# Instance norm over 268 MB of traffic: fp32 units kept on chip, with loads and stores in one queue

## The chip, the cores and the metric

The kernel runs on one core of a Trainium2 chip, and the other cores are idle. The metric is the device time of one execution in microseconds (us), as a median over several runs.

## The reference

```python
# x: (4, 8, 16, 256, 256) float32, gamma: (8, 16) float32
mu  = x.mean(axis=(3, 4), keepdims=True)
var = ((x - mu) ** 2).mean(axis=(3, 4), keepdims=True)
out = (x - mu) / np.sqrt(var + 1e-5) * gamma[None, :, :, None, None]
```

There are 512 channels of 65,536 values each. A channel has to be read whole before its first output is known. Since x is 134.22 MB and out is as large, at least 268.44 MB pass through the core's DMA engines, if x is read once.

## The kernel before

It takes 128 channels at a time, one to a partition. They come in as 2 MB pieces (rows of 16 KB) through four staging buffers. ACT copies each piece to a bf16 cache and sums it, and DVE sums its squares. When all 16 pieces are in, DVE scales the cache in place, and Pool issues stores that cast bf16 back to fp32.

```python
    # CW = 4096; staging has bufs=4; x_cache is [128, 65536] bf16, one buffer
    for ct in range(n_chtiles):                       # 4 tiles of 128 channels
        for j, (off, width) in enumerate(cur_p1):     # last tile ends in 4 pieces of 1024
            x_ck = staging.tile([P, CW], mybir.dt.float32, name="xck")
            nc.sync.dma_start(out=x_ck[:, :width], in_=x_flat[ch_lo:ch_hi, off : off + width])
            nc.scalar.activation(out=x_cache[:, off : off + width], in_=x_ck[:, :width],
                func=mybir.ActivationFunctionType.Copy, accum_out=sum_parts[:, j : j + 1])
            nc.vector.tensor_tensor_reduce(out=sq_scratch[:, :width], in0=x_ck[:, :width],
                in1=x_ck[:, :width], ..., accum_out=sq_parts[:, j : j + 1])
        # ... scale_ and shift_ from the sums: eight small instructions on DVE and ACT ...
        for j, (off, width) in enumerate(p2_chunks):  # 16 pieces
            nc.vector.tensor_scalar(out=x_cache[:, off : off + width], in0=..., scalar1=scale_[:],
                scalar2=shift_[:], op0=mybir.AluOpType.mult, op1=mybir.AluOpType.add)
            nc.gpsimd.dma_start(out=out_flat[ch_lo:ch_hi, off : off + width],
                                in_=x_cache[:, off : off + width])   # casts bf16 -> fp32
```

Of the kernel before, what the change touches and what calls it, by code (L numbers as in the profile page):

```python
# [1 line left out]

# [4 lines left out]


@with_exitstack  # L10
def kernel(
    ctx: ExitStack,
    tc: tile.TileContext,
    x: bass.AP,
    gamma: bass.AP,
    out: bass.AP,
):
    nc = tc.nc
    B, G, C, H, W = x.shape
    HW = H * W  # L20
    n_ch = B * G * C
    P = nc.NUM_PARTITIONS

    assert n_ch % P == 0
    assert G * C == P, "kernel assumes gamma broadcast exactly along partition dim"

    x_flat = x.rearrange("b g c h w -> (b g c) (h w)")
    out_flat = out.rearrange("b g c h w -> (b g c) (h w)")
    gamma_flat = gamma.rearrange("g c -> (g c)")

    n_chtiles = n_ch // P
    CW = 4096
    TAIL = 1024
    assert HW % CW == 0
    n_chunks = HW // CW
    p1_chunks = [(i * CW, CW) for i in range(n_chunks)]
    n_tail = CW // TAIL
    p1_chunks_last = [(i * CW, CW) for i in range(n_chunks - 1)] + [
        ((n_chunks - 1) * CW + i * TAIL, TAIL) for i in range(n_tail)
    ]  # L40
    p2_chunks = p1_chunks

    cache_dt = mybir.dt.bfloat16

    staging = ctx.enter_context(tc.tile_pool(name="staging", bufs=4))
    cache_pool = ctx.enter_context(tc.tile_pool(name="cache", bufs=1))
    singles = ctx.enter_context(tc.tile_pool(name="singles", bufs=1))
    scratch_pool = ctx.enter_context(tc.tile_pool(name="scratch", bufs=1))
    stats_pool = ctx.enter_context(tc.tile_pool(name="stats", bufs=2))

    g_tile = singles.tile([P, 1], mybir.dt.float32)
    nc.sync.dma_start(out=g_tile[:], in_=gamma_flat[:, None])  # L52

    eps_tile = singles.tile([P, 1], mybir.dt.float32)
    nc.vector.memset(eps_tile[:], 1e-5)  # L55

    x_cache = cache_pool.tile([P, HW], cache_dt)
    sq_scratch = scratch_pool.tile([P, CW], cache_dt)

    for ct in range(n_chtiles):  # L60
        ch_lo = ct * P
        ch_hi = ch_lo + P

        cur_p1 = p1_chunks_last if ct == n_chtiles - 1 else p1_chunks
        n_p1 = len(cur_p1)
        sum_parts = stats_pool.tile([P, n_p1], mybir.dt.float32, name="sum_parts")
        sq_parts = stats_pool.tile([P, n_p1], mybir.dt.float32, name="sq_parts")

        for j, (off, width) in enumerate(cur_p1):
            x_ck = staging.tile([P, CW], mybir.dt.float32, name="xck")  # L70
            nc.sync.dma_start(  # L71
                out=x_ck[:, :width], in_=x_flat[ch_lo:ch_hi, off : off + width]
            )
            nc.scalar.activation(  # L74
                out=x_cache[:, off : off + width],
                in_=x_ck[:, :width],
                func=mybir.ActivationFunctionType.Copy,
                accum_out=sum_parts[:, j : j + 1],
            )
            nc.vector.tensor_tensor_reduce(  # L80
                out=sq_scratch[:, :width],
                in0=x_ck[:, :width],
                in1=x_ck[:, :width],
                scale=1.0,
                scalar=0.0,
                op0=mybir.AluOpType.mult,
                op1=mybir.AluOpType.add,
                accum_out=sq_parts[:, j : j + 1],
            )

        sum_ = stats_pool.tile([P, 1], mybir.dt.float32, name="sum_")
        sq_sum_ = stats_pool.tile([P, 1], mybir.dt.float32, name="sq_sum_")
        nc.vector.reduce_sum(out=sum_[:], in_=sum_parts[:], axis=mybir.AxisListType.X)  # L93
        nc.vector.reduce_sum(out=sq_sum_[:], in_=sq_parts[:], axis=mybir.AxisListType.X)

        inv_n = 1.0 / HW
        tmp_ = stats_pool.tile([P, 1], mybir.dt.float32, name="tmp_")
        nc.vector.tensor_scalar(  # L98
            out=tmp_[:],
            in0=sum_[:],  # L100
            scalar1=sum_[:],
            scalar2=-inv_n,
            op0=mybir.AluOpType.mult,
            op1=mybir.AluOpType.mult,
        )
        nc.vector.tensor_add(out=sq_sum_[:], in0=sq_sum_[:], in1=tmp_[:])  # L106
        rstd_ = stats_pool.tile([P, 1], mybir.dt.float32, name="rstd")
        nc.scalar.activation(  # L108
            out=rstd_[:],
            in_=sq_sum_[:],  # L110
            func=mybir.ActivationFunctionType.Sqrt,
            bias=eps_tile[:],
            scale=inv_n,
        )
        nc.vector.reciprocal(out=rstd_[:], in_=rstd_[:])  # L115
        scale_ = stats_pool.tile([P, 1], mybir.dt.float32, name="scale")
        nc.vector.tensor_mul(out=scale_[:], in0=rstd_[:], in1=g_tile[:])  # L117
        shift_ = stats_pool.tile([P, 1], mybir.dt.float32, name="shift")
        nc.vector.tensor_scalar(  # L119
            out=shift_[:],  # L120
            in0=sum_[:],
            scalar1=-inv_n,
            scalar2=scale_[:],
            op0=mybir.AluOpType.mult,
            op1=mybir.AluOpType.mult,
        )

        for j, (off, width) in enumerate(p2_chunks):
            nc.vector.tensor_scalar(  # L129
                out=x_cache[:, off : off + width],  # L130
                in0=x_cache[:, off : off + width],
                scalar1=scale_[:],
                scalar2=shift_[:],
                op0=mybir.AluOpType.mult,
                op1=mybir.AluOpType.add,
            )
            nc.gpsimd.dma_start(  # L137
                out=out_flat[ch_lo:ch_hi, off : off + width],
                in_=x_cache[:, off : off + width],
            )  # L140


# [1 line left out]
_INS = ['x', 'gamma']  # L144
_OUTS = [((4, 8, 16, 256, 256), 'float32')]


# [23 lines left out]
```

## Time and profile before

| | before |
|---|---|
| measured, median of 3 runs (us) | 643.14 |
| span of the profile (us) | 641.5 |
| bytes over the DMA (MB) | 268.49 |
| DMA rate, loads only / both directions / stores only (GB/s) | 429 / 428 / 431 |
| DVE, ACT busy (share of the span) | 58%, 38% |

The first view is the page of the kernel before. The rows of digits have one place for each of 40 equal slices of the span, and a 9 means busy for 90% or more. GB/s is what the DMA engines moved in each slice. The last lines are groups of instructions: line, engine, operation, output<-input, count, then busy time and mean duration in ns, then the idle time just before them and what ended most of it.

```profile
span 641.5 us, 779 instructions
...
DVE 369.2 (58%) x227; ACT 241.7 (38%) x140; POOL 60.2 (9%) x68
...
DMA  8999999999999999999999999999999999599997
GB/s 355 429 430 428 429 426 430 430 429 426 431 428 427 429 427 433 431 427 430 428 429 427 427 429 429 392 440 425 426 426 433 431 425 426 230 425 441 425 436 316
...
q1 hardware_dynamic: 9792, 134.22, 55.0%
q0 software_dynamic: 9216, 134.22, 50.6%
...
L80 DVE CUSTOM_DVE_ANT_0 sq_scratch<-xck 128x4096 bf16<-128x4096 f32 (+1 forms) x67 | 283.6, 4233 | 201.5 <-DMA xck<-in_x_dram 201.0
L74 ACT ACTIVATE x_cache<-xck 128x4096 bf16<-128x4096 f32 (+1 forms) x67 | 232.0, 3463 | 301.4 <-issue 161.1
```

The DMA row is full almost everywhere, and the compute engines mostly wait for data: of DVE's 201.5 us of idle time before its square pass, a load ended 201.0. So the DMA engines bound the kernel.

The next view is a table of windows of the kernel before: from:to and length in us, busy time of DVE, ACT and Pool with instruction counts, the clock, the DMA share, and GB/s in the last column.

```profile
20.00:80.00 60.00, 54.47 (x25) 45.78 (x25) 0.00 (x0) 1.00 1.01 429
140.00:240.00 100.00, 46.32 (x21) 37.09 (x20) 1.59 (x3) 1.00 1.10 428
552.00:560.00 8.00, 7.28 (x16) 3.15 (x7) 1.67 (x2) 1.00 0.13 53
580.00:620.00 40.00, 0.00 (x0) 0.00 (x0) 2.65 (x5) 1.00 1.06 431
```

The rate hardly depends on the direction. In the third window the DMA share is 0.13: the engines have nothing to do for 7 of 8 us. The timeline of the kernel before (start, length, engine, line, operation, and in brackets the idle time before) says why:

```profile
553.38 1.22 DVE L80 CUSTOM_DVE_ANT_0 sq_scratch<-xck 128x1024 bf16<-128x1024 f32 x1
...
555.54 0.29 ACT L108 ACTIVATE rstd<-sq_sum__491,eps_tile 128x1 f32<-128x1 f32 x1 [0.68 <-DVE sq_sum__491 L106]
...
558.15 1.08 POOL L137 DMA_DIRECT2D out_dram<-x_cache  x1 [78.15 <-DVE x_cache L129]
```

The loads are over, and the last squares, the coefficients and the first scaled piece have to be done before the first store of the last tile can be issued at 558.15.

### The profile page before, as it was taken

How to read it: one execution, taken by the hardware profiler on the slowest of the kernel's cores; microseconds unless marked ns; L12 is line 12 of the kernel's file. 1: busy time of each engine (PE TensorE's matmuls, PEld its weight loads, DVE VectorE, ACT ScalarE, POOL GpSimd, SP SyncE). 2: the span in 40 equal slices, each digit the busy share in tenths (PEclk: the TensorE clock that was granted, in tenths of full speed). 3: DMA queues.
4: the chain of work that ended last, by engine and by line, in shares of the span. 5: the costliest groups of instructions: out<-in, count | busy, mean ns of one | idle time of the engine just before them, and what ended most of it. 6: DMA issues, size and time to landing. Idle time of an engine off the chain costs nothing.

```text
span 641.5 us, 779 instructions
## 1 busy us (share of the span) xinstructions
DVE 369.2 (58%) x227; ACT 241.7 (38%) x140; POOL 60.2 (9%) x68
## 2 busy tenths in 40 slices
DVE  4989999853443547993543534997435435690000
ACT  4777732624424332443343342263433434400000
POOL 0000033000000001500000000150000000150000
DMA  8999999999999999999999999999999999599997
GB/s 355 429 430 428 429 426 430 430 429 426 431 428 427 429 427 433 431 427 430 428 429 427 427 429 429 392 440 425 426 426 433 431 425 426 230 425 441 425 436 316
DMA packets 19015, 268.49 MB, mean 419 GB/s; under 512 B 2241, under 2 KB 2241, under 8 KB 2753
## 3 DMA queue, kind: packets, MB, share of 16 engines
q1 hardware_dynamic: 9792, 134.22, 55.0%
q0 software_dynamic: 9216, 134.22, 50.6%
q14 instruction: 7, 0.05, 0.0%
HBM read 134.22 MB, written 134.22 MB: 418 GB/s over the span
## 4 chain that ended last, share of the span: by engine, by line
issue 39%; DMA 34%; another core or an unknown queue 8%; DVE 7%; POOL 3%; ACT 1%; SPq 0%; POOLq 0%; DVEq 0%
DMA out_dram<-x_cache 19%; DMA xck<-in_x_dram 15%; DVE sq_scratch L80 4%; POOL out_dram L137 3%; DVE x_cache L129 3%; ACT x_cache L74 1%; SPq L71 0%; POOLq L166 0%; POOLq L137 0%; SPq L52 0%; ACT rstd L108 0%; DVE sq_parts L80 0%; DVE shift L119 0%; DVE rstd L115 0%
## 5 line engine op out<-in xcount | busy, mean ns | idle before, releaser
L80 DVE CUSTOM_DVE_ANT_0 sq_scratch<-xck 128x4096 bf16<-128x4096 f32 (+1 forms) x67 | 283.6, 4233 | 201.5 <-DMA xck<-in_x_dram 201.0
L74 ACT ACTIVATE x_cache<-xck 128x4096 bf16<-128x4096 f32 (+1 forms) x67 | 232.0, 3463 | 301.4 <-issue 161.1
L137 POOL DMA_DIRECT2D out_dram<-x_cache x64 | 60.0, 937 | 539.8 <-DVE x_cache L129 357.7
L129 DVE TENSOR_SCALAR x_cache<-x_cache,scale,shift 128x4096 bf16<-128x4096 bf16 x64 | 80.7, 1338 | 0.1
L74 ACT ACTIVATION_READ_ACCUMULATOR x_cache<-xck 128x1 f32 x67 | 12.5, 186 | 0.0
L80 DVE DVE_READ_ACCUMULATOR2_ANT sq_parts<- 128x1 f32 x67 | 5.5, 82 | 0.0
L108 ACT ACTIVATE rstd<-sq_sum__367,eps_tile 128x1 f32<-128x1 f32 x1 | 0.3, 295 | 6.3 <-DVE sq_sum__367 L106 6.3
L108 ACT ACTIVATE rstd<-sq_sum__255,eps_tile 128x1 f32<-128x1 f32 x1 | 0.3, 295 | 4.9 <-DVE sq_sum__255 L106 4.9
L93 DVE TENSOR_REDUCE sum__254<-sum_parts 128x1 f32<-128x16 f32 x1 | 0.2, 170 | 3.0 <-ACT x_cache L74 3.0
L74 ACT ACT_TABLE_LOAD x1 | 1.3, 1283 | 0.7 <-PEq L155 0.7
L115 DVE RECIPROCAL rstd<-rstd 128x1 f32<-128x1 f32 x4 | 0.7, 163 | 1.4 <-ACT rstd L108 1.4
L108 ACT ACT_TABLE_LOAD x1 | 1.3, 1283 | 0.0
L117 DVE TENSOR_TENSOR scale<-rstd,g_tile 128x1 f32<-128x1 f32 x4 | 0.6, 158 | 0.1
L108 ACT ACTIVATE rstd<-sq_sum__491,eps_tile 128x1 f32<-128x1 f32 x1 | 0.3, 295 | 0.7 <-DVE sq_sum__491 L106 0.7
L55 DVE MEMSET eps_tile<- 128x1 f32 x1 | 0.1, 59 | 0.8 <-PEq L155 0.8
L108 ACT ACTIVATE rstd<-sq_sum__143,eps_tile 128x1 f32<-128x1 f32 x1 | 0.3, 294 | 0.1
L98 DVE TENSOR_SCALAR tmp__494<-sum__490 128x1 f32<-128x1 f32 x1 | 0.2, 215 | 0.0
L119 DVE TENSOR_SCALAR shift<-sum__142,scale 128x1 f32<-128x1 f32 x1 | 0.2, 214 | 0.0
L119 DVE TENSOR_SCALAR shift<-sum__490,scale 128x1 f32<-128x1 f32 x1 | 0.2, 214 | 0.0
L98 DVE TENSOR_SCALAR tmp__258<-sum__254 128x1 f32<-128x1 f32 x1 | 0.2, 214 | 0.0
L119 DVE TENSOR_SCALAR shift<-sum__254,scale 128x1 f32<-128x1 f32 x1 | 0.2, 214 | 0.0
L119 DVE TENSOR_SCALAR shift<-sum__366,scale 128x1 f32<-128x1 f32 x1 | 0.2, 214 | 0.0
(17 smaller groups left out, 2.6 us busy)
## 6 DMA issues: line engine op xcount, KB each, us to landing
out_dram<-x_cache POOLq DMA_DIRECT2D x64, 2048.0 KB, 41.2
xck<-in_x_dram SPq DMA_DIRECT2D x63, 2048.0 KB, 24.0
xck<-in_x_dram SPq DMA_DIRECT2D x4, 512.0 KB, 14.7
g_tile<-in_gamma_dram SPq DMA_DIRECT2D x1, 0.5 KB, 2.1
```

Of the source, the lines that this page charges most:

```text
L55: nc.vector.memset(eps_tile[:], 1e-5)
L74: nc.scalar.activation(out=x_cache[:, off : off + width], in_=x_ck[:, :width], func=mybir.ActivationFunctionType.Copy, accum_out=sum_parts ...
L80: nc.vector.tensor_tensor_reduce(out=sq_scratch[:, :width], in0=x_ck[:, :width], in1=x_ck[:, :width], scale=1.0, scalar=0.0, op0=mybir.Alu ...
L93: nc.vector.reduce_sum(out=sum_[:], in_=sum_parts[:], axis=mybir.AxisListType.X)
L98: nc.vector.tensor_scalar(out=tmp_[:], in0=sum_[:], scalar1=sum_[:], scalar2=-inv_n, op0=mybir.AluOpType.mult, op1=mybir.AluOpType.mult,)
L108: nc.scalar.activation(out=rstd_[:], in_=sq_sum_[:], func=mybir.ActivationFunctionType.Sqrt, bias=eps_tile[:], scale=inv_n,)
L115: nc.vector.reciprocal(out=rstd_[:], in_=rstd_[:])
L117: nc.vector.tensor_mul(out=scale_[:], in0=rstd_[:], in1=g_tile[:])
L119: nc.vector.tensor_scalar(out=shift_[:], in0=sum_[:], scalar1=-inv_n, scalar2=scale_[:], op0=mybir.AluOpType.mult, op1=mybir.AluOpType.mult,)
L129: nc.vector.tensor_scalar(out=x_cache[:, off : off + width], in0=x_cache[:, off : off + width], scalar1=scale_[:], scalar2=shift_[:], op0= ...
L137: nc.gpsimd.dma_start(out=out_flat[ch_lo:ch_hi, off : off + width], in_=x_cache[:, off : off + width],)
```

## The change

The intent is to feed the DMA better. A unit is now 32 channels on 4 partitions each, 64 KB to a partition and 8 MB in all. Three units fit on chip in fp32, so no bf16 copy, no cast and no second buffer for the output are needed. DVE takes mean and variance with bn_stats. One small matmul averages them over the 4 partitions of a channel, and ACT scales the unit in place. Transfers are 4 MB with rows of 32 KB. After four loads at the start, stores and loads take turns in the SP queue. gamma now comes through ACT's queue.

```diff
-    CW = 4096
-    staging = ctx.enter_context(tc.tile_pool(name="staging", bufs=4))
-    x_cache = cache_pool.tile([P, HW], cache_dt)
+    S = 4;  K = P // S;  F = HW // S;  U = n_ch // K          # 16 units
+    CW = 8192;  NCK = F // CW                                 # 2 transfers to a unit
+    xv = x.rearrange("b g c h w -> (b g c h w)").rearrange("(u p f) -> u p f", p=P, f=F)
+    data = ctx.enter_context(tc.tile_pool(name="data", bufs=3 * NCK))
+    for u in range(2):
+        for j in range(NCK):
+            load(u, j)                                        # nc.sync.dma_start
 ... (matrix "avg" for the matmul, gamma spread over partitions) ...
-            nc.scalar.activation(... Copy, accum_out=sum_parts ...)
-            nc.vector.tensor_tensor_reduce(... accum_out=sq_parts ...)
+    # stats(u): 32 x nc.vector.bn_stats on 512 columns
+    # finalize(u, st): bn_aggr, matmul with avg, sqrt, reciprocal -> scale, shift
+    # emit(u, ...): for j in range(NCK): nc.scalar.activation(t, t, Identity, bias=shift, scale=scale)
-            nc.gpsimd.dma_start(out=out_flat[...], in_=x_cache[...])
+    coef = finalize(0, stats(0))
+    emit(0, *coef)
+    for u in range(U):
+        for j in range(NCK):
+            t = tiles.pop((u, j))
+            nc.sync.dma_start(out=ov[u, :, j * CW : (j + 1) * CW], in_=t[:])
+            if u + 2 < U:
+                load(u + 2, j)
+        if u + 1 < U:
+            coef = finalize(u + 1, stats(u + 1))
+            emit(u + 1, *coef)
```

More of the change, by code (lines that the diff above doesn't have):

```diff
@@ L7 @@
 from concourse._compat import with_exitstack
+F32 = mybir.dt.float32
+ALU = mybir.AluOpType
+ACTF = mybir.ActivationFunctionType
 @with_exitstack
@@ L19 @@
     B, G, C, H, W = x.shape
+    P = nc.NUM_PARTITIONS
     HW = H * W
     n_ch = B * G * C
-    P = nc.NUM_PARTITIONS
-    assert n_ch % P == 0
-    assert G * C == P, "kernel assumes gamma broadcast exactly along partition dim"
-    x_flat = x.rearrange("b g c h w -> (b g c) (h w)")
-    out_flat = out.rearrange("b g c h w -> (b g c) (h w)")
-    gamma_flat = gamma.rearrange("g c -> (g c)")
-    n_chtiles = n_ch // P
-    CW = 4096
-    TAIL = 1024
-    assert HW % CW == 0
-    n_chunks = HW // CW
@@ L36 @@
-    p1_chunks = [(i * CW, CW) for i in range(n_chunks)]
-    n_tail = CW // TAIL
-    p1_chunks_last = [(i * CW, CW) for i in range(n_chunks - 1)] + [
-        ((n_chunks - 1) * CW + i * TAIL, TAIL) for i in range(n_tail)
-    ]
-    p2_chunks = p1_chunks
-    cache_dt = mybir.dt.bfloat16
-    staging = ctx.enter_context(tc.tile_pool(name="staging", bufs=4))
-    cache_pool = ctx.enter_context(tc.tile_pool(name="cache", bufs=1))
+    S = 4
+    K = P // S
+    F = HW // S
+    U = n_ch // K
+    CW = 8192
@@ L47 @@
+    NCK = F // CW
+    FMAX = 512
+    NG = (G * C) // K
+    assert HW % S == 0 and F % CW == 0 and (G * C) % K == 0
+    xv = x.rearrange("b g c h w -> (b g c h w)").rearrange("(u p f) -> u p f", p=P, f=F)
+    ov = out.rearrange("b g c h w -> (b g c h w)").rearrange("(u p f) -> u p f", p=P, f=F)
+    gv = gamma.rearrange("g c -> (g c)")
+    data = ctx.enter_context(tc.tile_pool(name="data", bufs=3 * NCK))
     singles = ctx.enter_context(tc.tile_pool(name="singles", bufs=1))
-    scratch_pool = ctx.enter_context(tc.tile_pool(name="scratch", bufs=1))
@@ L49 @@
     stats_pool = ctx.enter_context(tc.tile_pool(name="stats", bufs=2))
-    g_tile = singles.tile([P, 1], mybir.dt.float32)
-    nc.sync.dma_start(out=g_tile[:], in_=gamma_flat[:, None])
-    eps_tile = singles.tile([P, 1], mybir.dt.float32)
-    nc.vector.memset(eps_tile[:], 1e-5)
-    x_cache = cache_pool.tile([P, HW], cache_dt)
-    sq_scratch = scratch_pool.tile([P, CW], cache_dt)
-    for ct in range(n_chtiles):
-        ch_lo = ct * P
-        ch_hi = ch_lo + P
-        cur_p1 = p1_chunks_last if ct == n_chtiles - 1 else p1_chunks
-        n_p1 = len(cur_p1)
-        sum_parts = stats_pool.tile([P, n_p1], mybir.dt.float32, name="sum_parts")
-        sq_parts = stats_pool.tile([P, n_p1], mybir.dt.float32, name="sq_parts")
-        for j, (off, width) in enumerate(cur_p1):
-            x_ck = staging.tile([P, CW], mybir.dt.float32, name="xck")
-            nc.sync.dma_start(
-                out=x_ck[:, :width], in_=x_flat[ch_lo:ch_hi, off : off + width]
-            )
-            nc.scalar.activation(
-                out=x_cache[:, off : off + width],
-                in_=x_ck[:, :width],
-                func=mybir.ActivationFunctionType.Copy,
-                accum_out=sum_parts[:, j : j + 1],
-            )
-            nc.vector.tensor_tensor_reduce(
-                out=sq_scratch[:, :width],
-                in0=x_ck[:, :width],
-                in1=x_ck[:, :width],
-                scale=1.0,
-                scalar=0.0,
-                op0=mybir.AluOpType.mult,
-                op1=mybir.AluOpType.add,
-                accum_out=sq_parts[:, j : j + 1],
-            )
-        sum_ = stats_pool.tile([P, 1], mybir.dt.float32, name="sum_")
-        sq_sum_ = stats_pool.tile([P, 1], mybir.dt.float32, name="sq_sum_")
-        nc.vector.reduce_sum(out=sum_[:], in_=sum_parts[:], axis=mybir.AxisListType.X)
-        nc.vector.reduce_sum(out=sq_sum_[:], in_=sq_parts[:], axis=mybir.AxisListType.X)
-        inv_n = 1.0 / HW
-        tmp_ = stats_pool.tile([P, 1], mybir.dt.float32, name="tmp_")
-        nc.vector.tensor_scalar(
-            out=tmp_[:],
-            in0=sum_[:],
-            scalar1=sum_[:],
-            scalar2=-inv_n,
-            op0=mybir.AluOpType.mult,
-            op1=mybir.AluOpType.mult,
-        )
-        nc.vector.tensor_add(out=sq_sum_[:], in0=sq_sum_[:], in1=tmp_[:])
-        rstd_ = stats_pool.tile([P, 1], mybir.dt.float32, name="rstd")
-        nc.scalar.activation(
-            out=rstd_[:],
-            in_=sq_sum_[:],
-            func=mybir.ActivationFunctionType.Sqrt,
-            bias=eps_tile[:],
-            scale=inv_n,
-        )
-        nc.vector.reciprocal(out=rstd_[:], in_=rstd_[:])
-        scale_ = stats_pool.tile([P, 1], mybir.dt.float32, name="scale")
-        nc.vector.tensor_mul(out=scale_[:], in0=rstd_[:], in1=g_tile[:])
-        shift_ = stats_pool.tile([P, 1], mybir.dt.float32, name="shift")
-        nc.vector.tensor_scalar(
-            out=shift_[:],
-            in0=sum_[:],
-            scalar1=-inv_n,
-            scalar2=scale_[:],
-            op0=mybir.AluOpType.mult,
-            op1=mybir.AluOpType.mult,
-        )
-        for j, (off, width) in enumerate(p2_chunks):
-            nc.vector.tensor_scalar(
-                out=x_cache[:, off : off + width],
-                in0=x_cache[:, off : off + width],
-                scalar1=scale_[:],
-                scalar2=shift_[:],
-                op0=mybir.AluOpType.mult,
-                op1=mybir.AluOpType.add,
-            )
-            nc.gpsimd.dma_start(
-                out=out_flat[ch_lo:ch_hi, off : off + width],
-                in_=x_cache[:, off : off + width],
-            )
@@ new lines, with load @@
+    psum = ctx.enter_context(tc.tile_pool(name="psum", bufs=2, space=bass.MemoryType.PSUM))
+    ctx.enter_context(tc.manual_schedule())
+    tiles = {}
+    def load(u, j):
+        t = data.tile([P, CW], F32, name="xt")
+        nc.sync.dma_start(out=t[:], in_=xv[u, :, j * CW : (j + 1) * CW])
+        tiles[u, j] = t
+    for u in range(2):
+        for j in range(NCK):
+            load(u, j)
+    g_row = singles.tile([1, G * C], F32, name="g_row")
+    nc.scalar.dma_start(out=g_row[:], in_=gv[None, :])
@@ new lines @@
+    eps_t = singles.tile([P, 1], F32, name="eps_t")
+    nc.vector.memset(eps_t[:], 1e-5)
+    avg = singles.tile([P, K, S], F32, name="avg")
+    nc.gpsimd.memset(avg[:], 1.0 / S)
+    nc.gpsimd.affine_select(
+        out=avg[:], in_=avg[:], pattern=[[-S, K], [0, S]], compare_op=ALU.is_ge,
+        fill=0.0, base=0, channel_multiplier=1,
+    )
+    nc.gpsimd.affine_select(
+        out=avg[:], in_=avg[:], pattern=[[S, K], [0, S]], compare_op=ALU.is_ge,
+        fill=0.0, base=S - 1, channel_multiplier=-1,
+    )
@@ new lines @@
+    one = singles.tile([1, 1], F32, name="one")
+    nc.vector.memset(one[:], 1.0)
+    g_rep = singles.tile([1, NG, K, S], F32, name="g_rep")
+    nc.vector.tensor_copy(
+        out=g_rep[:],
+        in_=g_row[:].rearrange("o (n k) -> o n k", n=NG).unsqueeze(3).to_broadcast([1, NG, K, S]),
+    )
+    g_ps = psum.tile([P, NG], F32, name="g_ps")
+    for n in range(NG):
+        nc.tensor.matmul(
+            out=g_ps[:, n : n + 1],
+            lhsT=g_rep[:, n].rearrange("o k s -> o (k s)"),
+            rhs=one[:],
+            start=True, stop=True,
+        )
@@ new lines, with stats, finalize @@
+    g_col = singles.tile([P, NG], F32, name="g_col")
+    nc.vector.tensor_copy(out=g_col[:], in_=g_ps[:])
+    def stats(u):
+        st = stats_pool.tile([P, F // FMAX, 6], F32, name="st")
+        for j in range(NCK):
+            for s in range(CW // FMAX):
+                nc.vector.bn_stats(
+                    out=st[:, j * (CW // FMAX) + s, :],
+                    in_=tiles[u, j][:, s * FMAX : (s + 1) * FMAX],
+                )
+        return st
+    def finalize(u, st):
+        mv = stats_pool.tile([P, 2], F32, name="mv")
+        nc.vector.bn_aggr(out=mv[:], in_=st[:].rearrange("p n s -> p (n s)"))
+        nc.vector.scalar_tensor_tensor(
+            out=mv[:, 1:2], in0=mv[:, 0:1], scalar=mv[:, 0:1], in1=mv[:, 1:2],
+            op0=ALU.mult, op1=ALU.add,
+        )
+        ps = psum.tile([P, 2], F32, name="ps")
+        nc.tensor.matmul(
+            out=ps[:], lhsT=avg[:].rearrange("p k s -> p (k s)"), rhs=mv[:],
+            start=True, stop=True,
+        )
+        cm = stats_pool.tile([P, 2], F32, name="cm")
+        nc.vector.tensor_copy(out=cm[:], in_=ps[:])
+        nmean = stats_pool.tile([P, 1], F32, name="nmean")
+        nc.vector.tensor_scalar(
+            out=nmean[:], in0=cm[:, 0:1], scalar1=-1.0, scalar2=None, op0=ALU.mult,
+        )
+        var = stats_pool.tile([P, 1], F32, name="var")
+        nc.vector.scalar_tensor_tensor(
+            out=var[:], in0=cm[:, 0:1], scalar=nmean[:], in1=cm[:, 1:2],
+            op0=ALU.mult, op1=ALU.add,
+        )
+        std = stats_pool.tile([P, 1], F32, name="std")
+        nc.scalar.activation(out=std[:], in_=var[:], func=ACTF.Sqrt, bias=eps_t[:], scale=1.0)
+        rstd = stats_pool.tile([P, 1], F32, name="rstd")
+        nc.vector.reciprocal(out=rstd[:], in_=std[:])
+        scale = stats_pool.tile([P, 1], F32, name="scale")
+        g = u % NG
+        nc.vector.tensor_mul(out=scale[:], in0=rstd[:], in1=g_col[:, g : g + 1])
+        shift = stats_pool.tile([P, 1], F32, name="shift")
+        nc.vector.tensor_mul(out=shift[:], in0=nmean[:], in1=scale[:])
+        return scale, shift
@@ new lines, in emit @@
+    def emit(u, scale, shift):
+        for j in range(NCK):
+            t = tiles[u, j]
+            nc.scalar.activation(
+                out=t[:], in_=t[:], func=ACTF.Identity, bias=shift[:], scale=scale[:],
+            )
+    coef = finalize(0, stats(0))
+    emit(0, *coef)
+    for u in range(U):
+        for j in range(NCK):
+            t = tiles.pop((u, j))
[5 more added lines that the diff above has]
+            emit(u + 1, *coef)
```

## The prediction

> **What bounds the kernel now.** The 16 DMA engines. The page counts 268.49 MB (134.22 read, 134.22 written) and 99% DMA busy in almost every one of the 40 slices; the table of windows gives 428 to 430 GB/s whether only loads run (10 to 80 us), both directions (140 to 240 us) or only stores (580 to 620 us). At 429 GB/s those bytes need 626 us of the 641.5 us span. The other 15 us are the start (first bytes at 2.6 us), 1.4 us of idle DMA near 414 us, about 7 us of idle DMA at 552 to 559 us (in the timeline: last loads, last statistics, first scaled chunk, first store issue), and about 4 us from the last bytes (637 us) to the end. DVE is busy 58%, ACT 38%: neither binds in the steady state. The Trainium skill ("DMA: Bandwidth & Descriptors", section "Where 436 GB/s comes from") puts the ceiling at 435 GB/s; the trace is already within 1.5% of it.
>
> **What the change does.** The bytes over the DMA do not change: the bf16 copy never saved HBM traffic, because loads and stores are fp32 on the HBM side. So the change can only win back parts of the 15 us and of the last 1.5% of rate.
> - Removes: the Pool-issued casting stores (60 us of POOL busy, off the path), the sum pass on ACT, the square pass on DVE.
> - Adds: 512 bn_stats of 512 fp32. From DVE's 1024-element reduction (1.22 us; 4096 take 4.42 us) I estimate 0.6 to 0.7 us each, 10 to 11 us for 4 MB, against 9.8 us per 4 MB of DMA. ACT scaling of 8192 fp32: from 3.62 us for 4096, an estimate of 7.1 us each. Per 8 MB unit: DVE about 24 us, ACT about 15 us, DMA 39 us. Both fit under the DMA.
> - Moves: loads and stores into one queue, in order. With three units, a load never waits for its buffer's store, which is some 40 us back; a store is ready roughly 10 to 20 us before the queue runs dry.
>
> **What is on the critical path.** Start: two units loaded by about 42 us, while unit 0's statistics (end about 34), its coefficients (about 3.5, with a hop through PE) and the first scaled chunk (7.1) let the first store move bytes at about 46 us: a new gap of about 4 us. Tail: the same chain after the last load (some 24 us) is covered by only two queued 4 MB stores (19.5 us): a gap of about 4 us, in place of 7. The 1.4 us gap goes. Sum: 2.6 + 625 + 4 + 4 + 4 = 640 us of span, 641 measured. Larger rows (32 KB instead of 16 KB) and no second queue may lift the rate a little, up to 1%; I take 2 us off.
>
> **Prediction:** 639 us, 8 in 10 between 632 and 646. Faster by over 2%: 0.05; within 2%: 0.91; slower by over 2%: 0.04.
>
> **What the profile would show.** Right: DMA share near 1.0 and 428 to 433 GB/s from 60 to 590 us; one dip of 3 to 5 us between 41 and 47 us and one about 35 to 45 us before the end; SP waiting for ACT, not for stores, at each turn; DVE busy near 330 us, ACT near 230 us. Wrong: a lower rate in the middle windows (turns between load and store cost bubbles), or dips repeating every 39 us (compute doesn't keep ahead).
>
> **What would make it wrong.** Bubbles at the 60 turns in one queue: 0.3 us each would add about 18 us. Or a rate of 434, which would save 7 us. Or bn_stats at 0.9 us, which would widen both gaps by about 3 to 5 us.

## The result, and the profile after

The changed kernel took 638.49 us (median of 4 runs, 637.51 to 638.71), against 643.11 us (4 runs) for the kernel before. A ratio in this document is the mean time of one kernel's fast runs over that of the other's fast runs of the same rounds, so it is not quite the ratio of the medians. Here it is 0.9927, with a 95% interval of 0.9913 to 0.9941: 0.7% faster, which is within the 2% that counts as the same.

| | before | after |
|---|---|---|
| span (us) | 641.5 | 636.7 |
| DMA rate in the middle, both directions (GB/s; before 140 to 240 us, after 100 to 580 us) | 428 | 432 |
| DVE busy (us) | 369.2 | 343.5 |
| ACT busy (us) | 241.7 | 235.1 |
| Pool busy (us) | 60.2 | 1.4 |

The page of the changed kernel, the same parts as above:

```profile
span 636.7 us, 965 instructions
...
PE 11.2 (2%) x40; PEld 9.8 (2%) x40; DVE 343.5 (54%) x644; ACT 235.1 (37%) x49; POOL 1.4 (0%) x7
...
DMA  9989999999999999999999999999999999999968
GB/s 379 441 365 389 406 436 428 436 428 437 432 426 432 434 428 434 434 426 433 428 438 432 430 432 430 429 435 428 438 432 434 429 430 437 432 432 434 430 266 362
...
q1 hardware_dynamic: 9216, 268.44, 98.3%
...
L95 DVE BATCH_NORM_STATS2 st<-xt 128x6 f32<-128x512 f32 x512 | 306.8, 678 | 239.3 <-DMA xt<-in_x_dram 239.2
L139 ACT ACTIVATE xt<-xt,shift,scale 128x8192 f32<-128x8192 f32 x32 | 229.1, 7206 | 9.9 <-DVE shift L133 9.9
```

The kernel is as DMA bound as before, and the rate is a little higher. The slices show two weak places: the third to fifth (365, 389, 406) and the last but one (266). The windows of the changed kernel (columns as above, with PE and its weight loads in front) measure them:

```profile
5.00:40.00 35.00, 0.56 (x2) 0.50 (x2) 25.63 (x48) 4.45 (x2) 0.00 (x0) 1.00 1.00 433
41.00:43.00 2.00, 0.00 (x0) 0.00 (x0) 2.00 (x5) 2.00 (x2) 0.00 (x0) 1.00 0.00 0
100.00:580.00 480.00, 7.06 (x24) 6.03 (x24) 262.14 (x489) 185.05 (x38) 0.00 (x0) 1.00 1.00 432
607.00:616.00 9.00, 0.00 (x0) 0.00 (x0) 0.48 (x3) 8.38 (x3) 0.00 (x0) 1.00 0.31 131
```

At 41 to 43 us nothing moves, and at 607 to 616 us only a third does. The timeline of the changed kernel gives the chain behind each:

```profile
12.94 19.31 DVE L95 BATCH_NORM_STATS2 st<-xt 128x6 f32<-128x512 f32 x32 [8.37 <-DMA xt<-in_x_dram]
...
35.85 14.32 ACT L139 ACTIVATE xt<-xt,shift,scale 128x8192 f32<-128x8192 f32 x2 [0.62 <-DVE shift L133]
43.09 0.35 SPq L149 DMA_DIRECT2D out_dram<-xt  x1
...
594.50 9.59 DVE L95 BATCH_NORM_STATS2 st<-xt 128x6 f32<-128x512 f32 x16 [9.77 <-DMA xt<-in_x_dram]
604.12 1.02 DVE L103 BATCH_NORM_AGGREGATE mv<-st 128x2 f32<-128x192 f32 x1
...
607.69 14.32 ACT L139 ACTIVATE xt<-xt,shift,scale 128x8192 f32<-128x8192 f32 x2 [0.62 <-DVE shift L133]
```

The four first loads are used up at about 41 us, but unit 0 is scaled far enough for its first store only at 43.09. At the end, the last load has landed at 594.5, its statistics take to 604, and its first half is scaled at about 614.9 (half of the 14.32 us after 607.69). Only two stores are queued to cover that.

### Sixteen engines, one landing

One part of the result can't be seen in the windows. The Trainium skill ("DMA: Bandwidth & Descriptors", section "Why a DMA increments its semaphore by 16 and not by 1") says that each of the 16 DMA engines that share a transfer adds one to the semaphore when its part has landed. The trace agrees: it holds 16 increments for every transfer of x. Their spread tells how far the engines have come apart, and since everything waits for the sixteenth, the last engine sets the time. These are increments in the changed kernel, as times from the start of the span (worked out from the trace's semaphore records):

```
transfer        first engine   median   last engine   spread (us)
1st landed          12.38       12.61      12.91          0.53
3rd                 31.80       32.04      32.34          0.54
33rd               327.34      327.73     331.54          4.20
58th               569.24      569.83     575.11          5.87
62nd               607.97      608.59     613.81          5.84
63rd (a store)     625.86      625.95     626.06          0.20
64th               635.57      635.64     635.74          0.17
```

(In the loads-only start of the kernel before the spread stays at 0.94 us from its first load to its twelfth, and in its stores at the end it stays at 0.16 to 0.21.) The first three landings of 4 MB, with nothing but loads running, follow each other every 9.71 us, and the spread does not grow. (The fourth comes 10.56 us after the third, with a spread of 1.38 us; a likely reason is given under act_stores.) Once both directions run, some engines fall behind. They only come together again at the end, when all of them wait for the same store to be issued.

With this the span can be split along the last engine. The time before the first landing less one transfer is the start (12.9 - 9.7 = 3.2), the time after the last landing is the end, and 64 transfers at 9.71 us are 621.4 us. The two dips are what the spacing of landings shows over 9.71: 2.65 us (42.90 to 55.26) and 2.54 us (613.81 to 626.06). What remains is the rest, which also holds any landing that came late outside the dips:

| span in us | start | 64 transfers | dips, last engine | end | rest | largest spread |
|---|---|---|---|---|---|---|
| after | 3.2 | 621.4 | 5.2 | 1.0 | 5.9 | 5.9 |

The kernel before, in the same way, with 128 transfers of 2 MB at 4.894 us in its loads-only part: start 4.1, transfers 626.4, end 3.4 (last landing 638.05), and 7.6 left for its idle DMA.

### The profile page after: what moved, and what is told of

Read it like the earlier page. It is cut to its first block, busy times and chain, and to the rows that moved or that the text cites. A ratio compares the mean times of both kernels' runs of the same rounds, so it can differ in the third digit from the quotient of the medians.

```text
span 636.7 us, 965 instructions
## 1 busy us (share of the span) xinstructions
PE 11.2 (2%) x40; PEld 9.8 (2%) x40; DVE 343.5 (54%) x644; ACT 235.1 (37%) x49; POOL 1.4 (0%) x7
## 2 busy tenths in 40 slices
DMA packets 9225, 268.50 MB, mean 422 GB/s; under 512 B 1025, under 2 KB 1026, under 8 KB 1026
## 4 chain that ended last, share of the span: by engine, by line
DMA 71%; DVE 11%; ACT 7%; issue 5%; ACTq 2%; PE 1%; SPq 0%
DMA xt<-in_x_dram 42%; DMA out_dram<-xt 30%; DVE st L95 9%; ACT xt L139 7%; ACTq L180 2%; DVE mv L103 1%; PE ps L110 1%; ACT std L126 0%; DVE var L121 0%; DVE mv L105 0%; DVE rstd L128 0%; DVE scale L131 0%; DVE cm L115 0%; DVE shift L133 0%; DVE nmean L117 0%
## 5 line engine op out<-in xcount | busy, mean ns | idle before, releaser
L95 DVE BATCH_NORM_STATS2 st<-xt 128x6 f32<-128x512 f32 x512 | 306.8, 678 | 239.3 <-DMA xt<-in_x_dram 239.2
L139 ACT ACTIVATE xt<-xt,shift,scale 128x8192 f32<-128x8192 f32 x32 | 229.1, 7206 | 9.9 <-DVE shift L133 9.9
L126 ACT ACTIVATE std<-var,eps_t 128x1 f32<-128x1 f32 x16 | 4.7, 294 | 375.7 <-DVE var L121 375.7
L110 PE MATMUL ps<-mv,avg 128*128 128x2 f32 x32 | 9.4, 363 | 592.3 <-DVE mv L105 592.3
L110 PEld LDWEIGHTS ps<-mv,avg 128*128 128x128 f32 x32 | 8.0, 312 | 593.6 <-DVE mv L105 564.3
L103 DVE BATCH_NORM_AGGREGATE mv<-st 128x2 f32<-128x192 f32 x16 | 16.4, 1022 | 0.6
L115 DVE COPY cm<-ps 128x2 f32<-128x2 f32 x16 | 2.6, 159 | 10.9 <-PE ps L110 10.9
L128 DVE RECIPROCAL rstd<-std 128x1 f32<-128x1 f32 x16 | 2.6, 164 | 6.6 <-ACT std L126 6.6
L121 DVE SCALAR_TENSOR_TENSOR var<-cm,nmean 128x1 f32<-128x1 f32 x16 | 3.5, 220 | 0.6
L105 DVE SCALAR_TENSOR_TENSOR mv<-mv 128x1 f32<-128x1 f32 x16 | 3.5, 219 | 0.6
```

The costliest lines, as they stand in the source:

```text
L95: nc.vector.bn_stats(out=st[:, j * (CW // FMAX) + s, :], in_=tiles[u, j][:, s * FMAX : (s + 1) * FMAX],)
L103: nc.vector.bn_aggr(out=mv[:], in_=st[:].rearrange("p n s -> p (n s)"))
L105: nc.vector.scalar_tensor_tensor(out=mv[:, 1:2], in0=mv[:, 0:1], scalar=mv[:, 0:1], in1=mv[:, 1:2], op0=ALU.mult, op1=ALU.add,)
L110: nc.tensor.matmul(out=ps[:], lhsT=avg[:].rearrange("p k s -> p (k s)"), rhs=mv[:], start=True, stop=True,)
L115: nc.vector.tensor_copy(out=cm[:], in_=ps[:])
L121: nc.vector.scalar_tensor_tensor(out=var[:], in0=cm[:, 0:1], scalar=nmean[:], in1=cm[:, 1:2], op0=ALU.mult, op1=ALU.add,)
```

## The experiments

Every experiment starts from the changed kernel unless it is said otherwise. "Middle" is the DMA rate between 100 and 580 us. Drift is the largest spread of one landing over its 16 engines. All kernels were correct except the copies. Each job timed the kernel before as well: 642.88 to 642.96 us.

### Load before store (load_first)

```diff
         for j in range(NCK):
+            if u + 2 < U:
+                load(u + 2, j)
             t = tiles.pop((u, j))
             nc.sync.dma_start(out=ov[...], in_=t[:])
-            if u + 2 < U:
-                load(u + 2, j)
```

> In each turn the load of unit u+2 is issued before the store of unit u, so that one more 4 MB transfer stands in the queue ahead of every store (5 loads before the first store, 3 stores after the last load). Theory 1 (the two dips of the changed kernel, 41 to 43.5 us and 607 to 615.5 us, are the compute chain from a landed unit to its first scaled chunk, which 39 us of queued loads or 19.5 us of queued stores do not cover): both dips go, 9 to 12 us less, 626 to 629 us measured, no dip of the DMA share between 5 and 625 us. Rival (the dips are costs of turning one queue from loads to stores and back, or of engines that drift apart): the dips stay, moved by 10 us, and the time stays within 3 us of 638.

Measured: 635.38 us (633.55 to 635.79), ratio to before 0.9877. Windows of this kernel, same columns:

```profile
41.00:43.00 2.00, 0.00 (x0) 0.00 (x0) 2.00 (x5) 2.00 (x2) 0.00 (x0) 1.00 1.18 508
100.00:580.00 480.00, 7.06 (x24) 6.03 (x24) 261.04 (x487) 176.54 (x37) 0.00 (x0) 1.00 1.00 432
607.00:616.00 9.00, 0.00 (x0) 0.00 (x0) 0.00 (x0) 4.60 (x1) 0.00 (x0) 1.00 0.95 408
```

(A window this short can read above the sustained rate: its DMA share reads 1.18 too.) Both dips are gone, as theory 1 said; the last engine's landings around the last load are 9.66 us apart. So the dips were the chain from a landed unit to its first store. But the time fell by 3 us and not by 9 to 12, which is where the rival had put it (within 3 us of 638); the dips decide between the two, since they went and did not move. In the split further below, 5.2 us of dips are gone and the rest is 1.9 us larger, with a drift of 8.9 us instead of 5.9. The expectation of the time failed. It had counted the idle time of the average engine (about 6 us at the end: 9 us at 131 instead of 432 GB/s), where only the last engine's 2.5 us counted, and it did not know of the drift.

### Rows of 16 KB (rows16k), stores from Pool (pool_stores), both (pool_stores_16k)

```diff
-    CW = 8192                                    # rows16k, pool_stores_16k
+    CW = 4096
-            nc.sync.dma_start(out=ov[...], ...)  # pool_stores, pool_stores_16k
+            nc.gpsimd.dma_start(out=ov[...], ...)
```

> The changed kernel with 4096 columns (16 KB rows, 2 MB transfers, 12 buffers) and all else alike. Theory A (the rate rose from 428 to 432 GB/s because rows of 32 KB halve the packets and their fixed cost): 428 to 429 GB/s between 100 and 580 us, 5 us more of transfer time. Theory B (it rose because stores no longer go through a second, Pool-fed queue): 432 GB/s stays. Both: the first scaled chunk comes 3.6 us earlier (ACT needs 3.6 instead of 7.2 us), so each of the two dips shrinks by about 3.6 us. So A says 635 to 638 us, B says 630 to 633 us.

> The changed kernel with its stores issued from Pool, rows still 32 KB, no cast. Theory A (row size sets the rate): 431 to 433 GB/s between 100 and 580 us. Theory B (the Pool-fed second queue costs it): 428 to 429 GB/s. Both: loads now run ahead of the stores until the buffers are full, so the start dip goes (6 loads before the first store); the tail after the last byte is 4 us instead of 2 if that part belongs to Pool's queue. Time 632 to 642 us.

> Both at once: 16 KB rows and stores from Pool, so the transfers are as in the kernel before except for the cast and the layout. Theory A and theory B both say 428 to 429 GB/s in the middle; if they add, it is as low as the kernel before and each of the two other runs lies between. If the rate stays at 432, neither is the cause and the cast from bf16 or the layout of the rows in memory (256 KB apart against 64 KB) is. Time 630 to 642 us.

| kernel | rows | stores from | middle (GB/s) | drift (us) | time (us) | ratio to before |
|---|---|---|---|---|---|---|
| changed | 32 KB | SP | 432 | 5.9 | 638.49 | 0.9927 |
| rows16k | 16 KB | SP | 431 | 9.7 | 638.27 | 0.9918 |
| pool_stores | 32 KB | Pool | 433 | 4.8 | 631.11 | 0.9817 |
| pool_stores_16k | 16 KB | Pool | 431 | 4.8 | 634.67 | 0.9871 |

Theory B falls: a Pool-fed second queue does not cost rate; the fastest of the four has one. Theory A holds for part of the 4 GB/s: 16 KB rows cost 1 to 2 GB/s, and 3.6 us with stores from Pool. (The edit halves the transfer along with the row, here and in every later run on row size, so no run tells a cost per row from a cost per transfer. "Rows" below stands for both.) The last run stayed at 431 instead of 428, so by the expectation something else is in play too, the cast or the layout. rows16k gave no clear saving: it has the largest drift of the four, 9.7 us, which probably ate what its smaller dips saved. The surprise is pool_stores, below the range that was expected for it: with the stores out of the loads' queue the kernel gains 7 us.

### The cast (cast_16k)

ACT writes a bf16 piece into a small buffer, and the store from Pool casts it back; the base is pool_stores_16k. To make room, one of the 12 buffers for x goes (`bufs=3 * NCK - 1`).

```diff
+            h = half.tile([P, CW], mybir.dt.bfloat16, name="h")
-            nc.scalar.activation(out=t[:], in_=t[:], ...)
-            nc.gpsimd.dma_start(out=ov[...], in_=t[:])     # in the main loop
+            nc.scalar.activation(out=h[:], in_=t[:], ...)
+            nc.gpsimd.dma_start(out=ov[...], in_=h[:])     # right behind it
```

> Stores from Pool with 16 KB rows, but ACT writes bf16 into a small buffer and the store casts it back to fp32, as in the kernel before; the layout stays that of the changed kernel. The same without the cast ran at 431 GB/s between 100 and 580 us and took 634.7 us. If the cast is the last part of the old 428 GB/s: 428 to 429 and 637 to 640 us. If the layout of the rows in memory is: 431 stays, and 633 to 636 us.

Measured: 428 GB/s in the middle and 638.18 us, both as the first alternative says. So the cast, and not the layout, is the remaining part of the old rate. Two other things change with it: a load's buffer comes free earlier, when ACT is done, and there is one buffer less. That the DMA engines were short of work does not show: their share between 100 and 580 us is 1.10, against 1.01 without the cast. The 3.5 us of time are therefore the cast's only as far as these two do not count.

### A second hardware queue (act_stores)

```diff
-            nc.sync.dma_start(out=ov[...], in_=t[:])
+            nc.scalar.dma_start(out=ov[...], in_=t[:])
```

> The changed kernel with its stores issued from ACT: a second queue, but a hardware one, no Pool. Theory D (what the changed kernel lost was that one queue takes turns: the 16 engines drift apart, up to 5.9 us between the first and the last engine of one landing, and everything waits for the last engine; with a second queue an engine always has work in one of the two): drift below 4 us, loads run ahead as with stores from Pool, no dip at 41 to 44 us, 432 to 434 GB/s in the middle, 628 to 632 us. Rival (Pool's own descriptors were what helped): drift near 6 us and 635 us or more.

Measured: 631.14 us (630.83 to 631.90), ratio 0.9817, 433 GB/s in the middle. Windows of this kernel:

```profile
41.00:43.00 2.00, 0.00 (x0) 0.00 (x0) 2.00 (x5) 2.00 (x2) 0.00 (x0) 1.00 1.18 508
100.00:580.00 480.00, 7.04 (x24) 6.01 (x24) 264.88 (x493) 181.50 (x37) 0.00 (x0) 1.00 1.00 433
```

The time is the same as with stores from Pool, so Pool's own descriptors are not what helped: the second queue is. The part about the drift failed. One engine still ends up 5.9 us behind; the other 15, however, stay within 1.3 us, where in one queue five engines lay more than 2 us behind at the end.

The trace suggests why one engine falls behind. Besides x, the DMA engines carry the program's own instructions, in blocks of 8 KB through a queue that the pages list as "instruction". The first line is from the page of act_stores, the second from that of copy_two_16k (a copy without compute, below):

```profile
q14 instruction: 8, 0.06, 0.0%
q14 instruction: 2, 0.02, 0.0%
```

In act_stores six such blocks are fetched before the tail, at 40.3, 142.5, 278.8, 298.8, 395.9 and 521.4 us (times from the trace's DMA records; the changed kernel has one at 40.3 us too, just before its late fourth landing). After all of them but that of 298.8, the spread grows by 0.84 to 0.98 us, against the landing two before; between the first stores and the tail it grows by as much at no other time. pool_stores shows the same after five of its six, with 0.75 to 0.82 us. copy_two_16k has two fetches, at 359.8 and 389.2 us, and its spread grows by 0.4 us at the landing after each. copy_two_queues has no fetch once it runs, and no such step. No run isolates this, so it is likely and not shown.

### Fewer changes of direction (turns_8mb)

```diff
         for j in range(NCK):
             nc.sync.dma_start(out=ov[...], in_=t[:])
-            if u + 2 < U:
-                load(u + 2, j)
+        if u + 2 < U:
+            for j in range(NCK):
+                load(u + 2, j)
```

> One queue as in the changed kernel, but two stores and then two loads: half as many changes of direction, transfers still 4 MB. Theory D in the form that each change of direction costs some engines a little: drift at the end 3 us instead of 5.9, 2 to 4 us less than the changed kernel (634.5 to 636.5), both dips as they were. Rival (each transfer, not each change of direction, makes the engines drift): 5.5 to 6.5 us drift, 638 us.

Measured: 637.56 us, drift 5.1 us. With half the changes of direction the drift is nearly as large and the gain is 0.9 us, so this form of theory D falls: it had put the drift at 3 us and the gain at 2 to 4. The drift is also below the rival's 5.5 to 6.5 us. The cost is not in proportion to the number of turns.

### The transfers alone (copy_only, copy_two_queues)

```diff
-    coef = finalize(0, stats(0)); emit(0, *coef)
-            (finalize, stats and emit in the loop)     # both: x is copied to out, wrong on purpose
-            nc.sync.dma_start(out=ov[...], in_=t[:])   # copy_two_queues only
+            nc.scalar.dma_start(out=ov[...], in_=t[:])
```

> Wrong result on purpose: no statistics and no scaling, x is copied to the output by the same 64 transfers in the same one queue and order. Theory D: the drift is a matter of the transfers alone, so it stays at 5 to 6 us or more while both dips go (5 us): 632 to 634 us. Rival (the drift comes from waiting on compute, or from DVE and ACT reading the same memory): drift below 2 us and 626 to 628 us.

> Wrong result on purpose: the copy of x without statistics or scaling once more, 64 transfers of 4 MB, with the stores issued from ACT's queue instead of the loads' queue. The copy in one queue took 632.5 us, 6.1 us of drift, and half of its engines ran 3.5 us behind the others. If one queue for both directions costs something of its own, whatever the compute does: 626 to 629 us, and only one engine far behind. Rival (the two-queue kernel gained 7 us over the changed kernel only because its loads run ahead and cover the dips): 631.5 to 633.5 us as in one queue.

The pages of both, first one queue, then two:

```profile
span 631.6 us, 137 instructions
...
GB/s 371 436 388 434 434 434 432 432 423 438 432 409 432 430 430 423 427 432 434 434 442 432 432 427 432 434 434 432 432 432 432 432 432 432 432 432 432 436 434 280
```

```profile
span 625.2 us, 190 instructions
...
GB/s 369 403 436 436 434 434 436 434 436 436 436 417 430 434 436 436 434 434 434 436 436 436 430 424 430 434 436 436 432 436 434 436 434 436 432 424 428 436 436 369
```

Measured: 632.49 us (631.06 to 633.53) in one queue and 627.04 us (626.64 to 627.40) in two. In one queue the drift grows to 6.1 us although no engine computes. In two queues it alternates between 0.8 and 2.1 us at the first pairs of transfers, and between 1.3 and 2.1 us at the last. So one queue for both directions costs about 5.5 us by itself, and compute is not needed for it. Nor did the one queue run dry: each transfer was issued at least 11 us before the fastest engine was done with the one before it. With this order of transfers, the copy in one queue, at 632.5 us, is already above the 631.1 us of the full kernel in two.

The split along the last engine, as above, for the kernels with 32 KB rows:

| span in us | start | 64 transfers | dips, last engine | end | rest | largest spread |
|---|---|---|---|---|---|---|
| after, 636.7 | 3.2 | 621.4 | 5.2 | 1.0 | 5.9 | 5.9 |
| turns_8mb, 636.4 | 3.1 | 621.4 | 4.2 | 1.0 | 6.7 | 5.1 |
| load_first, 633.4 | 3.2 | 621.4 | 0 | 1.0 | 7.8 | 8.9 |
| copy_only, 631.6 | 3.3 | 621.4 | 0 | 0.9 | 6.0 | 6.1 |
| act_stores, 629.5 | 3.2 | 621.4 | 0 | 1.5 | 3.3 | 5.9 |
| pool_stores, 629.2 | 3.1 | 621.4 | 0 | 2.1 | 2.5 | 4.8 |
| copy_two_queues, 625.2 | 3.1 | 621.4 | 0 | 0.9 | -0.2 | 2.2 |

(Each figure is rounded by itself. The first change of direction of copy_only and of load_first, 1.3 and 1.4 us over 9.71, is in their rest.) In the one-queue kernels the rest is within 2 us of the spread to which the engines drift. With two queues it is smaller than the spread, and with two queues and no compute it is gone. The one-queue drift is not all of one kind: in load_first four instruction fetches (137.7, 275.8, 393.3 and 519.8 us) are each followed by a step of 0.9 to 1.0 us, while copy_only has no fetch and drifts 6.1 us all the same.

### Row size without the rest (copy_two_16k, copy_two_64k, act_stores_64k)

```diff
-    CW = 8192
+    CW = 4096      # copy_two_16k, from copy_two_queues
+    CW = 16384     # copy_two_64k; act_stores_64k is act_stores with it
```

> Wrong result on purpose: the copy in two queues with 16 KB rows and 2 MB transfers. With 32 KB rows it took 627.0 us. If each row costs about 10 ns on its engine beside its bytes (loads alone landed every 4.89 us per 2 MB at 16 KB rows, every 9.71 us per 4 MB at 32 KB), 8192 more rows on 16 engines add 512 x 10 ns = 5 us: 631 to 633 us. Rival (row size does not matter, the changed kernel's rate came from dropping the cast alone): 626 to 628 us.

> The same with 64 KB rows and 8 MB transfers, three buffers. Row cost of 10 ns: 256 rows fewer on each engine, 2.5 us less, 624 to 626 us. Rival (32 KB was enough, or three large buffers starve a queue as in the kernel with 64 KB rows): 627 us or more, with dips in the DMA share.

> Stores from ACT, rows of 64 KB and transfers of 8 MB. If the rate in the middle follows from a fixed cost per row (431 GB/s at 16 KB, 433 at 32 KB), it is 434 to 435 GB/s between 100 and 580 us; if 32 KB was already enough, 433. The time says nothing of it: the chain from a landed unit to its first store grows to about 37 us (two passes of 9.6 us, 3.5 us of coefficients, 14.4 us of scaling), and only 19 to 30 us of stores cover it at the end, so 635 to 650 us with a dip near 600 us.

copy_two_16k took 630.07 us, with 431 GB/s in the middle: 3.0 us more than with 32 KB rows, not the expected 5. Rows of 16 KB do cost, but less with two queues than in a stream of loads alone. copy_two_64k took 632.71 us: 434 GB/s in the middle, but the engines drift 11.6 us apart. The second alternative holds for the time; that three buffers starved a queue is not shown, since the slices of the page dip only at the end (the last two read 299 and 337 GB/s). act_stores_64k is inconclusive: its runs went from 662.74 to 690.83 us, slower than expected. Its middle rate was 424 GB/s instead of 433 to 435, and no run shows why. 32 KB is the size that paid.

## Why the prediction was right

- **The bound.** Right. The DMA share is 1.00 and the rate 432 GB/s from 100 to 580 us. The prediction cited the Trainium skill's ceiling of 435 GB/s for this ("DMA: Bandwidth & Descriptors", section "Where 436 GB/s comes from"). The trace agrees: the highest middle rate of any run is 434 (copy_two_64k).
- **No bytes saved, so little time saved.** Right: 268.50 MB moved against 268.49.
- **Compute keeps ahead.** Right. There is no dip that repeats every 39 us. SP waited 569.7 us for ACT in all and 19.2 us for stores (the prediction had said that a load never waits for its buffer's store; it did 13 times, for 2.9 us at most), while the DMA had a backlog; this is the waits view of the DMA queue's own engine in the changed kernel (who waited for whom, total us, times, longest):

```profile
SPq L149 <- ACT xt L139: 569.7, 32, 40.4
SPq L51 <- DMA out_dram<-xt: 19.2, 13, 2.9
```

  The estimates of 10 to 11 us of bn_stats for 4 MB and 7.1 us of scaling were measured as 9.6 and 7.2 us. DVE's busy time was 343.5 us instead of about 330; it is off the path.
- **The two dips.** Right in cause (load_first removes both), and in place for the first (41 to 43 us). The second was put 35 to 45 us before the end and came 21 to 30 us before it, at 607 to 616 us. That was a slip within the prediction: its own sum leaves some 28 us after the gap begins, two stores of 9.75 us, a gap of 4 and an end of 4. Each dip cost 2.5 to 2.7 us on the last engine instead of 4. The lower bn_stats time accounts for part of it at the start. At the end the average engine idled longer than predicted, about 6 us, because the fast engines finished early.
- **The rate.** Right in direction and too small. The sum had 625 - 2 = 623 us for the bytes and 621.4 were measured; against the 626.4 of before the lift was 5 us and not 2. The prediction named larger rows and the missing second queue. These 5 us come from landings while only loads run, so they are the larger rows' alone (rows16k starts with 4.89 us per 2 MB, as before). With both directions the missing cast adds to it (428 to 431 GB/s). The missing second queue was a loss.
- **Start and end.** The sum carried 2.6 + 4 us over from before. Along landings they went from 4.1 + 3.4 to 3.2 + 1.0.
- **The turns in one queue.** The prediction listed 0.3 us at each of 60 turns as a risk (18 us) and put nothing for it into the sum. A cost is there: 5.9 us of rest, as drift of some engines and not as a bubble at every turn (turns_8mb). Not all of it need be the one queue's: act_stores keeps 3.3 us of rest in two queues.

In sum, 639 was close to 638.49 because a loss of 5.9 us that was left out met gains that were left out or taken too small: 2.8 us in the dips, 2.4 us at both ends and 1.6 us in the rate. The mechanism of the bound and of the dips is shown; the exact hit is partly luck.

Two things stay open. No run shows which DMA engines fall behind, nor why several do in one queue with no compute (copy_only); for the single engine of the two-queue kernels, instruction fetches are likely. And the runs do not separate how much of the 7.4 us between the changed kernel and act_stores is the dips and how much is the queue: load_first puts the dips at 3.1 us in one queue, the copies put the queue at 5.5 us.

## What to carry to other kernels

When a kernel moves its bytes at the full rate of the DMA engines, look for the remaining per cent at the ends (what is queued while the first and the last unit are computed) and in the spread of one landing over the 16 engines. Try a queue each for loads and stores even if one queue never runs dry: in the copies that was worth 5.5 us, and in the full kernel that one word, with nothing else changed, took the time from 638.5 to 631.1 us, 1.8% below the kernel before. Count an idle dip on the engine that lands last, since idle time of engines that were early is not time saved when the dip goes.

## What the Trainium skill lacked or had wrong

- "DMA: Bandwidth & Descriptors", sections "Issuing engines are not separate DMA queues" and "Rules for kernel authors": they say that issuing from several engines only saves the sequencer's issue time and does not help bandwidth. With the same 64 transfers of 4 MB, stores from ACT instead of SP took 627.04 us instead of 632.49, 0.9% less, although the issue time was covered in the one queue: each transfer was issued at least 11 us before the fastest engine needed it (copy_only).
- The same page, section "Latency and other measured facts", names two engines that are usually slower and ties this, as a best guess, to the rings of descriptors that software writes. Here one engine fell 5.9 us behind with hardware queues alone (act_stores); no run shows whether it is one of those two. No page says that the 16 engines drift apart when loads and stores mix: up to 8.9 us in one queue with 32 KB rows, against a constant 0.94 us in the loads-only part of the kernel before. Nor does one give the price of an instruction fetch to the engine that carries it: steps of 0.84 to 0.98 us follow five of six in act_stores.
- The same page, section "Bandwidth", gives about 10.5 ns per packet in a note on small transfers. The landings fit that for large rows: 4 MB took 2 x 4.894 us in 16 KB rows and 9.71 us in 32 KB rows, 0.078 us for 8 rows fewer on each engine, 9.8 ns a row, if none of it is the cost of the second transfer. The rule of 1 MiB or more to a transfer (section "Rules for kernel authors") does not tell that rows beyond 16 KB, in transfers beyond 2 MB, still pay: 3.0 us of 627 in copy_two_16k.
- No page has the price of a cast from bf16 to fp32 in a store: 431 to 428 GB/s in the middle, 634.67 to 638.18 us.
